# Attention scores of two heads side by side on TensorE's row halves, and a finer interleave of projections with the attention steps

## The chip, the cores and the metric

One Trainium2 chip, one of its cores. The metric is the device time of one execution in microseconds (us); the kernel before has a median of 945.48 us over 3 runs (945.21 to 947.18).

## The reference, cut to what matters

The kernel computes a decoder trunk of two layers on 256 tokens with 1024 channels. Each layer is a half-step SwiGLU, a mixer of three branches, and a second SwiGLU; the change lies in the mixer.

```python
h = rms_norm(x, norm_mix[l])
qa, ka, va, qb, kb, vb, xc, gc = _split_cols(h @ w_in[l])
# A: 4 query heads, 2 key heads of 64 channels, window 128, a sink per head
out_a = swa_sink_mixer(rope(qa), rope(ka), va, attn_sinks[l])
# B: 6 heads of 64 channels, three dilated windows joined by their denominators
out_b = dilated_mixer(rope(qb), rope(kb), vb)
# C: conv(4) -> gated linear recurrence, times gelu(gc)
out_c = rglru_mixer(xc, gc, conv_w[l], ..., positions)
x = x + concat(out_a, out_b, out_c) @ w_out[l]
```

In A and B every head computes `softmax(q k^T * scale + mask) v`, with 64 channels in the product q k^T.

## The kernel before, in words

All weights come as float32. `piece` (L123) loads a piece over SP's DMA queue, and splits it into two parts: ScalarE (ACT) makes `hi` (L130), VectorE (DVE) makes `lo` (L132). The same split is made of the activations by `split` (L135). Every product with weights is three TensorE (PE) matmuls in the one-pass format fp32r: hi x hi, hi x lo, lo x hi (L427 to L430 in `mac`, L461 to L463 in the SwiGLU, L704 to L706 in `project_T`, L938 to L940 in `out_stage`). Seven pieces fit in the ring of hi and lo tiles (tag "w", 14 tiles), so a new hi waits for the matmuls of the seventh piece before it.

What is computed inside the attention is plain float32, which the trace shows as two PE records for each matmul: the scores (L826), the product with the values (`o`, L856), and the recurrence gates (`gate_c`, L738). Transposes (`pT` L850, `qkT` L805, `gT` L437) are one record each.

One layer's mixer takes these steps, and the string `PLAN` (L20) is the order in which they are recorded:

- `xc`, `qb`, `kb`, `vb`, `pa`, `gc`: projections of the normed input: C's input, B's queries, keys and values, A's queries with keys and values, C's gate. They use 24 matmuls of 256 columns for each third of 384 channels (xc, gc), or 48 of 384 (qb, kb, vb) or 512 columns (pa).
- `cg`, `cs`, `co`: the gates, the scan and the output of C.
- `B0s0`, `A1s1` and so on: the scores of one group of heads for token half 0 or 1 (128 queries against 128 or 256 keys). `p` steps transpose the exponentials (pT), copy them out of PSUM on ACT (L657) and multiply with the values (o). `f` (`finish`, L859) divides by the sum, transposes (gT) and splits the result into `parts` (hi on ACT L136, lo on DVE L137).
- `woB`, `woCA`: the output projection over B's channels, then over C's and A's, in two halves of 512 output channels each (the loop over `c` in `out_stage`, L924), added to x by DVE (L943).

Behind the scores of a head stands a chain: DVE adds the mask and takes the maximum (L830), makes the negative maximum (L834, L836), ACT takes the exponential with the row sum (L839), and PE transposes. A head's 64 channels lie on one half of the partitions: even heads of B and key head 0 of A on partitions 0 to 63, the others on 64 to 127. Before, a group of scores is one bank of PSUM and holds heads of one half only:

```python
for g in range(2):
    for i0 in range(0, NP, per):
        heads.append([hd(2 * i + g) for i in range(i0, min(i0 + per, NP))])
```

A scheduler takes the recorded order as a priority and moves an instruction ahead where its inputs and its buffers allow. Each engine then runs its own list strictly in order. PSUM has 8 banks: 4 with the tag "mm", 2 "at", 2 "tp" (transposes).

Of the kernel before, what the change touches and what calls it, by code (L numbers as in the profile page):

```python
# [38 lines left out]
def hybrid_trunk(ctx: ExitStack, tc: tile.TileContext, a: dict, out: bass.AP):  # L39
# [393 lines left out]
    def gT(h, g, n, hi, lo):  # L433

        ps = bank("tp", "gT")
        for j in range(n // P):
            nc.tensor.transpose(ps[:, j * P:(j + 1) * P], g[:, j * P:(j + 1) * P], ident)  # L437
        split(hi, lo, ps[:, :n].rearrange("p (k t) -> p k t", t=P))
# [198 lines left out]
    def mixer(l, norm, nxt):  # L637
# [46 lines left out]

        def project(o, n, name):
            bs = None
            for k, w in w_in_pieces(o, n):
                if bs is None:
                    bs = [bank("mm", name)[:, :n] for _ in range(NH)]
                with behind_stats(k):  # L690
                    mac([(k, [(norm.parts(h, k), [(bs[h], w)]) for h in range(NH)])], KD)
            return bs

        def project_T(o, n, name, tags):

            bs = None
            for k, (wh, wl) in w_in_pieces(o, n):
                if bs is None:
                    bs = [bank(t, name)[:, :S] for t in tags]
                xh, xl = (norm.both(k)[:, o:o + S] for o in (0, S))  # L700
                with behind_stats(k):
                    for i, b in enumerate(bs):
# [3 lines left out]
                        nc.tensor.matmul(b, wj, xh, start=False, stop=(k == KD - 1))  # L706
# [13 lines left out]
        def c_conv():  # L720
            xc = project_T(oC, CW, "xc", TAG_XC)
# [41 lines left out]
        def c_gelu():  # L763
            gc = project_T(oC + CW, CW, "gc", TAG_GC)
# [3 lines left out]
            A.activation(ge, ge, AF.Gelu_apprx_tanh)  # L768
# [31 lines left out]
        def q_k(ps, h, nh, dst, groups=None):  # L800
            r = rope(ps, h, nh, groups)
            n = nh * HD // P
            tp = bank("tp", "qkT")
            for c in range(n):
                nc.tensor.transpose(tp[:, c * P:(c + 1) * P], r[:, c * P:(c + 1) * P], ident)  # L805
            copy("qk", dst[:, :, h * P:(h + 1) * P], tp[:, :n * P].rearrange("p (c t) -> p c t", c=n))

        class Attend:


            def __init__(self, h, heads, vs, mask, sinks):
                self.h, self.heads, self.vs, self.mask, self.sinks = h, heads, vs, mask, sinks
                self.nk = (h + 1) * P
                self.nh = sum(len(b) for b in heads)
                st = act.tile([P, 4, 8], F32, tag="st", bufs=4, name="st")
                self.mx, self.nm, self.ls, self.ri = (st[:, i] for i in range(4))
                self.slot = [sum(len(b) for b in heads[:i]) for i in range(len(heads))]
                self.sm = [None] * len(heads)
                self.ob = None

            def scores(self, gi):
                group, j, nk, mx, nm = self.heads[gi], self.slot[gi], self.nk, self.mx, self.nm
                h, n = self.h, len(group)
                sb = bank(TAG_SCORES, "scores")
                for s, (i, g, q, k) in enumerate(group):
                    nc.tensor.matmul(sb[:, s * nk:(s + 1) * nk], q[g * HD:(g + 1) * HD, h * P:(h + 1) * P],  # L826
                                     k[g * HD:(g + 1) * HD, :nk], start=True, stop=True)
                sm = act.tile([P, 512], F32, tag="sm", bufs=NSM, name="sm")
                for s in range(n):
                    V.tensor_tensor_reduce(out=sm[:, s * nk:(s + 1) * nk], in0=sb[:, s * nk:(s + 1) * nk],  # L830
                                           in1=self.mask, scale=1.0, scalar=NEG, op0=ALU.add, op1=ALU.max,
                                           accum_out=mx[:, j + s:j + s + 1])
                if self.sinks is None:
                    V.tensor_scalar(nm[:, j:j + n], mx[:, j:j + n], -SC, None, op0=ALU.mult)  # L834
                else:
                    V.scalar_tensor_tensor(nm[:, j:j + n], mx[:, j:j + n], -SC, self.sinks[1][:, j:j + n],  # L836
                                           op0=ALU.mult, op1=ALU.min)
                for s in range(n):
                    A.activation(sm[:, s * nk:(s + 1) * nk], sm[:, s * nk:(s + 1) * nk], AF.Exp, scale=SC,  # L839
                                 bias=nm[:, j + s:j + s + 1], accum_out=self.ls[:, j + s:j + s + 1])  # L840
                self.sm[gi] = sm

            def pv(self, gi):
                h, sm = self.h, self.sm[gi]
                if self.ob is None:
                    self.ob = bank(TAG_O, "o")
                tp = bank("tp", "pT")
                n = len(self.heads[gi]) * self.nk
                for b in range(n // P):
                    nc.tensor.transpose(tp[:, b * P:(b + 1) * P], sm[:, b * P:(b + 1) * P], ident)  # L850
                pT = act.tile([P, 512], F32, tag="pT", bufs=2, name="pT")
                copy("pT", pT[:, :n], tp[:, :n])
                for s, (i, g, q, k) in enumerate(self.heads[gi]):
                    for kb in range(h + 1):
                        b = s * (h + 1) + kb
                        nc.tensor.matmul(self.ob[:, i * HD:(i + 1) * HD], pT[:, b * P:(b + 1) * P], self.vs[kb][i],  # L856
                                         start=(kb == 0), stop=(kb == h))

            def finish(self):  # L859
# [7 lines left out]
                order = [i for group in self.heads for i, *_ in group]  # L867
# [155 lines left out]
```

## Time and profile before

| | us |
|---|---|
| median of 3 runs | 945.48 |
| the profiled execution: its own time | 946.71 |
| its span, first to last instruction | 944.9 |
| PE busy in the span | 935.2 (99%) |
| DVE busy | 662.1 (70%) |
| ACT busy | 502.0 (53%) |
| mean granted PE clock | 0.996 of full speed |

The two mixers lie at about 192 to 291 us and 654 to 753 us of the span. In them DVE is the fullest engine beside PE: the profile's stretches of 5 us show it busy for 5.00 of 5 us from 220 to 235 us, and for 2.30 of 5 us from 255 to 260 us. A busy time of PE is the sum of records whose ends are modelled: a matmul of 256 columns is shown as 0.28 us long although the next one starts 0.11 us later. So costs on PE are read from the distance of starts, and not from the length of a record.

### The profile page before, as it was taken

The numbers are of one execution on the slowest core, as the hardware profiler recorded it, in microseconds if no ns is written. First come the engines' busy times: TensorE is split into PE (matmuls) and PEld (weight loads), VectorE is DVE, ScalarE is ACT, GpSimd is POOL, SyncE is SP. The second block draws the span as 40 slices with busy tenths as digits, with TensorE's granted clock in tenths as the row PEclk, the third lists the DMA queues.
The fourth block names the chain that finished last, engine by engine and source line by source line (L and its number), as shares of the span: only waits on it lengthen the run. The fifth ranks groups of instructions, "written<-read, shape, count | busy, mean of one in ns | idle before, by whom it ended". The sixth has DMA issues, their size and how long they took to land.

```text
span 944.9 us, 18771 instructions
## 1 busy us (share of the span) xinstructions
PE 935.2 (99%) x7572; PEld 910.7 (96%) x7572; DVE 662.1 (70%) x1155; ACT 502.0 (53%) x769; POOL 59.8 (6%) x107
## 2 busy tenths in 40 slices
PE   8999999999999999999999999999999999999997
PEld 8999999999899999999999999999988999999886
DVE  6786675989678867765577766565995975656544
ACT  7554554455667545555355555544475675555530
POOL 4000001011102000001000000011100100000000
PEclk9999999999999999999999999999999999999999
DMA  8876665655246666565746666654741755666631
GB/s 279 238 227 206 191 197 162 195 175 166 79 132 214 178 205 198 180 216 165 223 157 200 194 205 203 202 180 119 224 138 50 229 178 180 196 207 201 201 112 44
DMA packets 134408, 171.13 MB, mean 181 GB/s; under 512 B 5822, under 2 KB 106258, under 8 KB 134322
## 3 DMA queue, kind: packets, MB, share of 16 engines
q1 hardware_dynamic: 133184, 168.32, 58.0%
q0 software_dynamic: 528, 0.57, 0.4%
q8 instruction: 59, 0.97, 0.4%
q10 hardware_dynamic: 608, 1.06, 0.4%
q14 instruction: 29, 0.22, 0.1%
HBM read 168.88 MB, written 1.05 MB: 180 GB/s over the span
## 4 chain that ended last, share of the span: by engine, by line
PE 97%; issue 1%; DMA 1%; SPq 0%; DVE 0%; POOLq 0%; POOL 0%
PE gate L461 9%; PE gate L462 9%; PE gate L463 8%; PE up L462 8%; PE up L463 8%; PE up L461 8%; PE down L461 6%; PE down L463 6%; PE down L462 6%; PE down L609 2%; PE down L608 2%; PE down L607 2%; PE scores L826 2%; PE wout L938 2%; PE wout L939 2%; PE wout L940 2%
## 5 line engine op out<-in xcount | busy, mean ns | idle before, releaser
L132 DVE TENSOR_TENSOR lo<-raw,hi 128x1024 fp32r<-128x1024 f32 (+2 forms) x334 | 388.8, 1173 | 113.7 <-ACT hi L130 113.3
L130 ACT ACTIVATE hi<-raw 128x1024 fp32r<-128x1024 f32 (+2 forms) x334 | 335.5, 1017 | 167.4 <-PE down L462 60.9
L461 PE MATMUL gate<-x,hi 128*128 128x256 f32 x704 | 195.8, 278 | 0.5 <-ACT x L372 0.5
L462 PE MATMUL gate<-x,hi 128*128 128x256 f32 x704 | 195.1, 277 | 0.0
L461 PE MATMUL up<-x,hi 128*128 128x256 f32 x704 | 194.6, 277 | 0.0
L462 PE MATMUL up<-x,hi 128*128 128x256 f32 x704 | 194.5, 277 | 0.0
L463 PE MATMUL gate<-x,lo 128*128 128x256 f32 x704 | 194.5, 277 | 0.0
L463 PE MATMUL up<-x,lo 128*128 128x256 f32 x704 | 194.1, 276 | 0.0
L461 PE MATMUL down<-g,hi 128*128 128x256 f32 x528 | 145.8, 276 | 0.0
L462 PE MATMUL down<-g,hi 128*128 128x256 f32 x528 | 145.7, 276 | 0.0
L463 PE MATMUL down<-g,lo 128*128 128x256 f32 x528 | 145.6, 276 | 0.0
L461 PEld LDWEIGHTS gate<-x,hi 128*128 128x128 f32 x704 | 132.6, 188 | 0.7 <-ACT x L372 0.7
L462 PEld LDWEIGHTS gate<-x,hi 128*128 128x128 f32 x704 | 132.8, 189 | 0.0
L462 PEld LDWEIGHTS up<-x,hi 128*128 128x128 f32 x704 | 132.4, 188 | 0.0
L463 PEld LDWEIGHTS gate<-x,lo 128*128 128x128 f32 x704 | 132.3, 188 | 0.0
L461 PEld LDWEIGHTS up<-x,hi 128*128 128x128 f32 x704 | 132.3, 188 | 0.0
L463 PEld LDWEIGHTS up<-x,lo 128*128 128x128 f32 x704 | 132.0, 188 | 0.0
L136 ACT ACTIVATE g<-gu 128x256 fp32r<-128x256 f32 x88 | 36.6, 417 | 149.3 <-DVE gu L475 125.4
L461 PEld LDWEIGHTS down<-g,hi 128*128 128x128 f32 x528 | 99.1, 188 | 0.1
L462 PEld LDWEIGHTS down<-g,hi 128*128 128x128 f32 x528 | 99.1, 188 | 0.0
L463 PEld LDWEIGHTS down<-g,lo 128*128 128x128 f32 x528 | 99.0, 188 | 0.0
L474 DVE TENSOR_TENSOR gu<-up,half 128x256 f32<-128x256 f32 x66 | 27.7, 421 | 47.1 <-PE up L463 47.1
(228 smaller groups left out, 1325.5 us busy)
## 6 DMA issues: line engine op xcount, KB each, us to landing
raw<-ffn_down SPq DMA_DIRECT2D x88, 512.0 KB, 4.5
raw<-ffn_gate SPq DMA_DIRECT2D x87, 512.0 KB, 4.7
raw<-ffn_up SPq DMA_DIRECT2D x87, 512.0 KB, 5.2
raw<-w_in SPq DMA_DIRECT2D x40, 384.0 KB, 3.7
raw<-w_out SPq DMA_DIRECT2D x12, 512.0 KB, 3.7
raw<-w_in SPq DMA_DIRECT2D x8, 512.0 KB, 4.6
raw<-w_out SPq DMA_DIRECT2D x8, 256.0 KB, 2.8
xr<-x SPq DMA_DIRECT2D x4, 256.0 KB, 4.6
```

The costliest lines, as they stand in the source:

```text
L130: nc.scalar.activation(hi[:, :m], raw[:, :m], AF.Copy)
L132: nc.vector.tensor_tensor(lo[:, :m], raw[:, :m], hi[:, :m].bitcast(F32), op=ALU.subtract)
L136: nc.scalar.activation(hi, v, AF.Copy)
L461: nc.tensor.matmul(b, wh, both[:, :S], start=first, stop=False)
L462: nc.tensor.matmul(b, wh, both[:, S:], start=False, stop=False)
L463: return nc.tensor.matmul(b, wl, both[:, :S], start=False, stop=last)
L474: V.tensor_tensor(u, bs[1], half, op=ALU.mult)
L607: nc.tensor.matmul(b, gh, wh, start=first, stop=False)
L608: nc.tensor.matmul(b, gh, wl, start=False, stop=False)
L609: return nc.tensor.matmul(b, gl, wh, start=False, stop=last)
L826: nc.tensor.matmul(sb[:, s * nk:(s + 1) * nk], q[g * HD:(g + 1) * HD, h * P:(h + 1) * P], k[g * HD:(g + 1) * HD, :nk], start=True, stop=True)
L938: nc.tensor.matmul(bs[j], wi, PT[:, k, 0], start=(i == 0), stop=False)
```

## The change

- **Scores by pairs.** `Attend` takes steps in place of groups. A step has two banks, one for each half of the partitions, and its matmuls are recorded in turn: a head of the lower half, one of the upper half, and so on. B has one step for half 0 (6 heads) and two for half 1 (4 and 2 heads); A has one step for each half (4 heads). The exponentials are laid out by head number in tiles of 512 columns, so `finish` needs no reordering, and the negative maximum is taken once for a step.
- **Steps cut finer.** `p` now only transposes and copies, `o` multiplies with the values, `aT` transposes A's rotated queries and keys. `project`, `project_T` and `out_stage` are generators, so one projection can be recorded in parts between other steps. `gl` is the gelu of C's gate, which was part of `gc`.
- **Order.** `behind(C["pe"])` holds matmuls and transposes of the attention behind the last projection matmul recorded before them. `PLAN` now has A's projection (`pa`) ahead of B's values (`vb`), and parts of `pa`, `vb`, `gc` and `wo` between the steps of the attention.
- **Banks.** `o` moves from the tag "at" to "mm", C's gate projection to "mm" alone, and the output projection to two "mm" and two "at" banks.

The arithmetic is unchanged. The core of the diff:

```diff
-PLAN = ("xc qb kb cg B1s0 vb B0s0 B0s1 B0p0 B0p1 pa B1s2 B1s1 cs A0s0 B1s3 B1p0 B0f A0s1 B1p2 B1p1 A1s0 B1p3 "
-        "A1s1 A0p1 A0p0 gc A1p0 B1f woB A1p1 A0f A1f co woCA").split()
-TAG_GATE, TAG_SCORES, TAG_O, TAG_WO = 'at', 'at', 'at', 'mm'
-TAG_XC, TAG_GC = ('mm', 'at', 'mm'), ('at', 'mm', 'mm')
+PLAN = ("xc qb kb cg pa pa pa B0s0 pa B1s0 vb B0p0 B0p1 B1s1 cs vb aT0 vb aT1 A0s0 vb gc B0o0 B0o1 B1p0 B1p1 "
+        "gc B1o0 B1o1 B1p2 B0f gc B1o2 A0p0 A1s0 gc gl A0o0 B1f A1p0 A1p1 woB A1o0 A1o1 A0f woB A1f co "
+        "woCA woCA woCA woCA").split()
+TAG_GATE, TAG_SCORES, TAG_O, TAG_WO = 'at', 'at', 'mm', ('mm', 'mm', 'at', 'at')
+TAG_XC, TAG_GC = ('mm', 'at', 'mm'), ('mm', 'mm', 'mm')
...
         def project(o, n, name):
             bs = None
             for k, w in w_in_pieces(o, n):
+                if k and k % 2 == 0:
+                    yield
...
             def scores(self, gi):
-                group, j, nk, mx, nm = self.heads[gi], self.slot[gi], self.nk, self.mx, self.nm
-                h, n = self.h, len(group)
-                sb = bank(TAG_SCORES, "scores")
-                for s, (i, g, q, k) in enumerate(group):
-                    nc.tensor.matmul(sb[:, s * nk:(s + 1) * nk], q[g * HD:(g + 1) * HD, h * P:(h + 1) * P],
-                                     k[g * HD:(g + 1) * HD, :nk], start=True, stop=True)
...
+                (banks, tiles), nk, mx, nm, h = self.steps[gi], self.nk, self.mx, self.nm, self.h
+                sb = [bank(TAG_SCORES, "scores") for _ in banks]
+                at = {}
+                for s in range(max(len(b) for b in banks)):
+                    for t, group in zip(sb, banks):
+                        if s < len(group):
+                            i, g, q, k = group[s]
+                            at[i] = t[:, s * nk:(s + 1) * nk]
+                            with behind(C["pe"]):
+                                nc.tensor.matmul(at[i], q[g * HD:(g + 1) * HD, h * P:(h + 1) * P],
+                                                 k[g * HD:(g + 1) * HD, :nk], start=True, stop=True)
...
+            def pT(self, gi):
+                sm, heads = self.sm[gi]
+                tp = bank("tp", "pT")
+                n = len(heads) * self.nk
+                for b in range(n // P):
+                    with behind(C["pe"]):
+                        nc.tensor.transpose(tp[:, b * P:(b + 1) * P], sm[:, b * P:(b + 1) * P], ident)
+                pT = act.tile([P, 512], F32, tag="pT", bufs=2, name="pT")
+                copy("pT", pT[:, :n], tp[:, :n])
+                self.p[gi] = pT
...
         def b_attend(h, q, k):
             hd = lambda i: (i, i % 2, q[:, i // 2], k[:, i // 2])
             per = 512 // ((h + 1) * P)
-            heads = []
-            for g in range(2):
-                for i0 in range(0, NP, per):
-                    heads.append([hd(2 * i + g) for i in range(i0, min(i0 + per, NP))])
-            return Attend(h, heads, vb, K["mB"][h], None)
+            steps = []
+            for i0 in range(0, NP, per):
+                pairs = range(i0, min(i0 + per, NP))
+                banks = [[hd(2 * i + g) for i in pairs] for g in range(2)]
+                idx = range(2 * i0, 2 * pairs[-1] + 2)
+                steps.append((banks, [list(idx[i:i + per]) for i in range(0, len(idx), per)]))
+            return Attend(h, steps, vb, K["mB"][h], None)
```

How the instructions now stand, at two places (layer 0; layer 1 has the same order). A row is a line of the kernel, the operation, output<-inputs with the buffer's number, and the shape; `xN` is N of them in a row.

**Place 1: PE, B's first scores.** Before, inside A's projection; the two tiles hold heads of the lower half only:

```order
L430 MATMUL pa_3086<-hi_3075,x_2019 128x512
L826 MATMUL scores_2944<-mixed_2597 128x256 x2
L826 MATMUL scores_3031<-mixed_2597 128x128 x3
L427 MATMUL pa_3087<-hi_3075,x_2019 128x512
L428 MATMUL pa_3087<-lo_3076,x_2019 128x512
```

Now all six heads of half 0 stand together, scores_3006 of the lower and scores_3007 of the upper half:

```order
L431 MATMUL pa_2957<-hi_2983,x_2522 128x512
L849 MATMUL scores_3006<-mixed_2597 128x128
L849 MATMUL scores_3007<-mixed_2597 128x128
L849 MATMUL scores_3006<-mixed_2597 128x128
L849 MATMUL scores_3007<-mixed_2597 128x128
L849 MATMUL scores_3006<-mixed_2597 128x128
L849 MATMUL scores_3007<-mixed_2597 128x128
L428 MATMUL pa_2956<-hi_2989,x_2522 128x512
```

The halves now take turns. In the whole mixer the scores stand in 9 unbroken runs before and in 7 now: B half 0 (the six above); B half 1, four in turn; the last two heads of B half 1, each alone between projections; A half 0 in the order lower, lower, upper, upper; A half 1, three in turn; and its last head alone.

**Place 2: PE, ACT and DVE, from B's last result to the output projection.** PE before: behind the transpose of B's result for half 1 (gT_3431) come one pair of transposes and 24 matmuls of gc, and only then wout:

```order
L850 MATMUL pT_3417<-ident_67,sm_3276 128x128 x2
L437 MATMUL gT_3431<-ident_67,o_3429 128x128 x3
L850 MATMUL pT_3417<-ident_67,sm_3276 128x128 x2
L704 MATMUL gc_3325<-x_2019,hi_3314 128x256
L705 MATMUL gc_3325<-x_2019,hi_3314 128x256
L706 MATMUL gc_3325<-x_2019,lo_3315 128x256
```

PE now: behind the same transpose (gT_3406) come four products of A and four transposes:

```order
L721 MATMUL gc_3235<-x_2522,lo_3301 128x256
L439 MATMUL gT_3406<-ident_67,o_3404 128x128 x3
L887 MATMUL o_3398<-va_3041,pT_3357 128x64 x4
L874 MATMUL pT_3412<-ident_67,sm_3365 128x128 x4
L971 MATMUL wout_3438<-parts_2598,hi_3427 128x256
L971 MATMUL wout_3439<-parts_2598,hi_3427 128x256
L971 MATMUL wout_3440<-parts_2598,hi_3427 128x256
L971 MATMUL wout_3441<-parts_2598,hi_3427 128x256
L874 MATMUL pT_3419<-ident_67,sm_3366 128x128 x4
L972 MATMUL wout_3438<-parts_2598,hi_3427 128x256
```

ACT now, where L866 is the exponential, L131 a weight's hi and L137 the hi of `parts`:

```order
L866 ACTIVATE sm_3365,st_3062<-sm_3365,st_3062 128x256 x2
L866 ACTIVATE sm_3366,st_3062<-sm_3366,st_3062 128x256 x2
L894 ACTIVATE st_3062<-st_3062 128x4
L131 ACTIVATE hi_3585<-raw_3584 128x1024
L137 ACTIVATE parts_2598<-gT_3406 128x3x128
L1014 ACT_TABLE_LOAD
```

DVE now, where L782 are C's gate products, L898 the division of A's half 0, L133 a weight's lo and L138 the lo of `parts`:

```order
L782 TENSOR_TENSOR ge_2599<-gc_3235,rows_2704 128x256
L898 TENSOR_TENSOR o_3495<-o_3398,st_3061 128x256
L895 TENSOR_TENSOR st_3062<-st_3062 128x4
L896 RECIPROCAL st_3062<-st_3062 128x4
L133 TENSOR_TENSOR lo_3586<-raw_3584,hi_3585 128x1024
L138 TENSOR_TENSOR parts_2598<-gT_3406,parts_2598 128x3x128
```

The first four wout matmuls read the hi of `parts`, the row L972 its lo; both now stand on ACT and DVE behind the exponentials of A's half 1 and behind a weight piece.

## Rows read from the trace of the kernel before

**Rows 1.** The page: busy times by engine, then the chain's shares.

```profile
PE 935.2 (99%) x7572; PEld 910.7 (96%) x7572; DVE 662.1 (70%) x1155; ACT 502.0 (53%) x769; POOL 59.8 (6%) x107
...
PE 97%; issue 1%; DMA 1%; SPq 0%; DVE 0%; POOLq 0%; POOL 0%
```

**Rows 2.** All waits of PE: who waited <- for whom: us, times, longest.

```profile
PE warm L115 <- POOL ident masks.py:199: 1.4, 1, 1.4
PE xT L367 <- DMA xr<-x: 1.1, 1, 1.1
PE gate L461 <- ACT x L372: 0.5, 1, 0.5
```

**Rows 3.** Groups by line: PE's scores (busy us, mean ns, idle before).

```profile
L826 PE MATMUL scores<-mixed 64*128 64x256 f32 (+1 forms) x80 | 17.8, 347 | 0.0
```

**Rows 4.** Timeline of PE (start, length): one score of 256 keys alone.

```profile
253.43 0.28 PE L706 MATMUL gc<-x,lo 128*128 128x256 f32 x1
253.63 0.70 PE L826 MATMUL scores<-mixed 64*128 64x256 f32 x2
254.26 0.39 PE L704 MATMUL gc<-x,hi 128*128 128x256 f32 x1
254.48 0.28 PE L705 MATMUL gc<-x,hi 128*128 128x256 f32 x1
```

**Rows 5.** The chain in order of time (start us, us, what): small PE work.

```profile
223.82 0.43 PE gate_c L738 x2
...
252.56 0.44 PE pT L850 x4
...
265.07 0.33 PE gT L437 x3
...
277.22 0.84 PE o L856 x8
```

**Rows 6.** Timeline of PE: from B's last transpose to the output projection.

```profile
264.90 0.49 PE L437 MATMUL gT<-ident,o 128*128 128x128 f32 x3
...
265.37 0.36 PE L704 MATMUL gc<-x,hi 128*128 128x256 f32 x1
...
268.16 0.28 PE L706 MATMUL gc<-x,lo 128*128 128x256 f32 x1
268.28 0.63 PE L938 MATMUL wout<-parts,hi 128*128 128x256 f32 x4
```

**Rows 7.** ACT in 192:300, groups by line and shape (busy, mean ns, idle).

```profile
L130 ACT ACTIVATE hi<-raw 128x1024 fp32r<-128x1024 f32 x19 | 19.5, 1052 | 7.4 <-PE pb L428 3.6 <-PE wout L939 3.3 <-ACT hi L130 0.2
L839 ACT ACTIVATE sm<-sm,st 128x256 f32<-128x256 f32 x10 | 5.0, 502 | 5.7 <-DVE st L834 5.7
L839 ACT ACT_TABLE_LOAD x1 | 1.3, 1283 | 0.0
L136 ACT ACTIVATE parts<-gT 128x384 fp32r<-128x384 f32 x2 | 1.0, 492 | 1.5 <-PE gT L437 1.5
```

**Rows 8.** DVE in 192:300, groups by line and shape.

```profile
L132 DVE TENSOR_TENSOR lo<-raw,hi 128x1024 fp32r<-128x1024 f32 x18 | 22.3, 1254 | 2.1 <-ACT hi L130 2.1
L830 DVE CUSTOM_DVE_ANT_0 sm<-scores,mA 128x256 f32<-128x256 f32 x4 | 1.5, 422 | 1.5 <-PE scores L826 1.5
L137 DVE TENSOR_TENSOR parts<-gT,parts 128x384 fp32r<-128x384 f32 x2 | 1.1, 558 | 0.6 <-ACT parts L136 0.6
L869 DVE TENSOR_TENSOR o<-o,st 128x256 f32<-128x256 f32 x2 | 0.8, 418 | 0.3 <-issue 0.3
```

**Rows 9.** Timeline of PE: two stretches of wout, first and last row each.

```profile
272.65 0.28 PE L938 MATMUL wout<-parts,hi 128*128 128x256 f32 x1
...
274.01 0.28 PE L938 MATMUL wout<-parts,hi 128*128 128x256 f32 x1
...
287.01 0.28 PE L938 MATMUL wout<-parts,hi 128*128 128x256 f32 x1
...
290.19 0.28 PE L938 MATMUL wout<-parts,hi 128*128 128x256 f32 x1
```

More of the change, by code (lines that the diff above doesn't have):

```diff
@@ L431, in mac, with gT @@
         return last
[L433 removed]
+    def gT(h, g, n, hi, lo, after=None):
         ps = bank("tp", "gT")
         for j in range(n // P):
[L437 removed]
+            with behind(after):
+                nc.tensor.transpose(ps[:, j * P:(j + 1) * P], g[:, j * P:(j + 1) * P], ident)
         split(hi, lo, ps[:, :n].rearrange("p (k t) -> p k t", t=P))
@@ L683, in behind_stats, with whole @@
             return behind(C.get("stats"))
+        def whole(g):
+            while True:
+                try:
+                    next(g)
+                except StopIteration as e:
+                    return e.value
         def project(o, n, name):
@@ L690, in project @@
                 with behind_stats(k):
-                    mac([(k, [(norm.parts(h, k), [(bs[h], w)]) for h in range(NH)])], KD)
+                    C["pe"] = mac([(k, [(norm.parts(h, k), [(bs[h], w)]) for h in range(NH)])], KD)
             return bs
@@ L813, in __init__ @@
                 self.nk = (h + 1) * P
-                self.nh = sum(len(b) for b in heads)
+                self.nh = sum(len(b) for banks, _ in steps for b in banks)
                 st = act.tile([P, 4, 8], F32, tag="st", bufs=4, name="st")
                 self.mx, self.nm, self.ls, self.ri = (st[:, i] for i in range(4))
-                self.slot = [sum(len(b) for b in heads[:i]) for i in range(len(heads))]
-                self.sm = [None] * len(heads)
+                self.sm, self.p = [], {}
@@ L843, in pv @@
             def pv(self, gi):
-                h, sm = self.h, self.sm[gi]
+                h, (_, heads), pT = self.h, self.sm[gi], self.p[gi]
                 if self.ob is None:
                     self.ob = bank(TAG_O, "o")
[L847 to L851, printed above, removed]
@@ L852, in pv @@
-                copy("pT", pT[:, :n], tp[:, :n])
-                for s, (i, g, q, k) in enumerate(self.heads[gi]):
+                for s, i in enumerate(heads):
                     for kb in range(h + 1):
                         b = s * (h + 1) + kb
-                        nc.tensor.matmul(self.ob[:, i * HD:(i + 1) * HD], pT[:, b * P:(b + 1) * P], self.vs[kb][i],
-                                         start=(kb == 0), stop=(kb == h))
+                        with behind(C["pe"]):
+                            nc.tensor.matmul(self.ob[:, i * HD:(i + 1) * HD], pT[:, b * P:(b + 1) * P],
+                                             self.vs[kb][i], start=(kb == 0), stop=(kb == h))
@@ L931, in out_stage @@
                 w = list(w.items())
-                bs = [bank(TAG_WO, "wout")[:, :S] for _ in range(KC)]
+                bs = [bank(TAG_WO[j], "wout")[:, :S] for j in range(KC)]
                 order = [(i, j) for i in range(n - LO) for j in range(KC)]
                 order += [(i, j) for j in range(KC) for i in range(n - LO, n)]
-                for i, j in order:
+                for ij, (i, j) in enumerate(order):
+                    if ij and ij == (n - LO) * KC:
+                        yield
                     k, (wh, wl) = w[i]
@@ L950, in out, with go_on @@
         def out(stage):
-            out_stage([R[m] for m in stage], stage == PLAN[-1][2:])
+            return out_stage([R[m] for m in stage], stage == PLAN[-1][2:])
+        running = {}
+        def go_on(step, start):
+            if step not in running:
+                running[step] = start()
+            next(running[step], None)
         for step in PLAN:
```

91 lines of the change are left out of this document (51 added, 40 removed).

## The prediction

> **What bounds the kernel now.** I read the page first. PE is busy for 99% of the span and is 97% of the chain that ended last [rows 1], so the end moves only if PE has less to do or is made to wait. The waits view then says whether it waits: three times in the whole program, 3.0 us in all, and all three at the very start [rows 2]. In neither mixer does PE wait for anyone as far as the records show, and no load of w_in or w_out is among the releasers. Since a record's end is modelled, I checked this with the distances of starts. A score of 256 keys costs two records (80 for 40 heads [rows 3]), a float32 matmul of 256 columns 0.43, four transposes 0.44 or three 0.33, four products with the values 0.84 [rows 5]. Added up over the mixer, such prices leave no gap over about 0.2 us at one place. So the attention already costs what PE's work in it costs: nothing is hidden that an interleave could uncover, and only the scores get cheaper. What the interleave can do is go wrong.
>
> One thing PE pays for that is no arithmetic: around a lone score of 256 keys, the starts from the gc matmul ahead to the second gc matmul behind are 254.48 - 253.43 = 1.05 us apart [rows 4]. Two steps of gc are 0.23 of it (such a matmul takes 0.113 to 0.118 [rows 9]), the score's columns 0.43 (the price of gate_c, of the same columns on all 128 rows [rows 5]). The other 0.39 is paid for going into the 64-row form and out of it. The score itself, on half the rows, streams no faster than a matmul on all of them.
>
> Durations below come from the profiled execution, which took 946.71 us with a span of 944.9; it lies 0.13% above the median of 945.48. I work out differences from it and put them on the median. About 0.2% (1.9 us) is what a measurement of this kernel can tell from no change.
>
> **Fewer runs of scores.** 9 runs a layer become 7. At 0.39 each that is 0.78 a layer, -1.6 us for both. I take it whole, since a run pays on the two sides whatever it holds.
>
> **Overlap of the halves.** Per layer the scores have 6x128 + 6x256 + 4x128 + 4x256 = 3840 columns, at 0.43 / 256 that is 6.45 us. No run of scores in the kernel before holds heads of both halves, so no row shows whether two of them run at once. One bound is nothing gained. For the other I count with two rules: a head's two records follow each other on its half, and records start in program order, but the next one may start beside the last if its half is free. A record is then 0.107 (128 keys) or 0.213 us (256), and n heads in turn take 2n + 1 steps in place of 4n/2 x 2: the six heads of B half 0 take 7 for 12 (saved 5 x 0.107 = 0.54), the four of half 1 take 5 for 8 (3 x 0.213 = 0.64), A half 0 in the order lower, lower, upper, upper 7 for 8 (0.11), the three of A half 1 take 4 for 6 (0.43). The three heads that stand alone save nothing. Sum 1.72 a layer, -3.4 us for both. I take this end: the two sets of rows, and the two banks written, have nothing in common, and rows 4 show that a score occupies the array's time for its columns, whichever half it leaves empty.
>
> On the loss side, a change of half inside a run may cost like the entry of a run; that is a rival below. The Trainium skill (TensorEngine Tiling (Array Packing), Key Properties) says that changing the tiling mode drains TensorE, while changing only the tile does not. The 0.39 of rows 4 agrees with the first half; no row here shows the second. By that rule the sum below stands as it is; if a change of half cost the 0.39 of the rows too, it would be the last rival's.
>
> **Out-projection, woB.** Here I find a wait that was not there. T is the end of A's last lone score on PE. Before, 24 gc matmuls stood between B's transpose and wout: 265.37 to 268.28 [rows 6], 2.9 us in which ACT (0.49) and DVE (0.56) made `parts`. Now there are four products (0.84) and four transposes (0.44).
> PE: 18 gc at 0.115 = 2.1, gT 0.33, o 0.84, pT 0.44, so it asks for wout at T + 3.7.
> ACT: the exponentials need the one negative maximum of all four heads, so they begin after DVE's last maximum (0.42) and some 0.2 of small steps, at T + 0.7; four take 4 x 0.50 [rows 7], to T + 2.7, one small exponential to T + 2.9, then the weight piece hi_3585 at 1.05 to T + 3.9, then the hi of `parts` 0.49 to T + 4.4. PE waits 0.7 and runs four wout matmuls (0.46), to T + 4.85.
> DVE: o_3495 waits for the four products (T + 3.3), 0.42, two small ones 0.3, lo_3586 1.25 to T + 5.3, the lo of `parts` 0.56 [rows 8] to T + 5.8. It holds up pT_3419 too, whose bank is the one that gT_3406 leaves. PE waits another 0.95.
> That is about 1.6 a layer; durations on ACT and DVE overlap a little at their ends, so I take 1.5, +3.0 us for both. Ends: none if the two engines come through earlier, 2.2 a layer if one more small step is late on each.
>
> **First exponentials.** B half 0's now stand on ACT behind two table loads (1.28 each [rows 7]), a square root and two weight pieces that wait for PE's last pa matmuls, and pT_3106 follows after 12 + 13 vb and one run of scores. My walk along ACT gives a margin between -0.4 and +0.7 us. I take 0.2 a layer, +0.4 us; ends 0 and 0.8.
>
> **Pace of the 256-column matmuls.** In one stretch of wout 12 matmuls take 274.01 - 272.65 = 1.36 (0.113 each), in a later one 27 take 290.19 - 287.01 = 3.18 (0.118) [rows 9]. Small work between seems to set which pace follows; I don't know the rule. Some 220 matmuls a layer ran at the slow pace and 57 of wout at the fast. All slow would cost 0.3 a layer, all fast would gain 1.0; I take the middle, -0.7 us for both.
>
> **Costs nothing.** The moved banks: `o` needs an "mm" bank that values or B's division leave; between those and its use stand 3 to 4 us of other PE work (22 gc at 0.115 for B half 1). The values' copies have 4 us from the last vb matmul to the first `o`. A's rotation and POOL's additions end some 8 us ahead of `aT0`. On SP's queue four loads of A's weights move ahead of vb's; PE waits for none of these loads now [rows 2], and hi pieces wait for PE instead. DVE has a few small maxima fewer and no reordering; PE's work covers that, it gives nothing. The cover is gone only where `parts` is late, above. The gelu apart from gc puts a table load behind the hi of `parts` and ahead of pT_3417's copy, which PE asks for 3.7 us later.
>
> **Sum.** -1.6 - 3.4 + 3.0 + 0.4 - 0.7 = -2.3 us, 945.5 - 2.3 = **943.2 us**.
>
> **The rivals.**
> *No wait at woB.* If ACT and DVE run further ahead than I walk them, 3.0 + 0.4 less one small rest fall away: -5.3, 940.2 us. For it: DVE had idle time in the attention before, 2.7 us of the 5 from 255 to 260. Against: the order of the rows on ACT and DVE is fixed. 0.17.
> *The halves do not overlap.* Only the runs count: -1.6 + 3.0 + 0.4 - 0.7 = +1.1, 946.6 us. For it: no row shows overlap. 0.15.
> *The halves are independent of program order.* Each half streams its own heads: B half 0 6 steps, B half 1 4, A half 0 4: another 0.64 a layer, 1.3 less: 941.9 us. For it: nothing in the rows; against: everything else on PE starts in order. 0.10. The Trainium skill (TensorEngine Tiling (Array Packing), Theoretical Speedup) gives up to 2x for 64 rows, which is this case where both halves are full; no run here shows it.
> *Weight loads set the pace.* Four products of 64 columns take 0.84, 0.21 each [rows 5], twice their columns' 0.107: loading float32 weights for a record takes about 0.105. If loads for the two halves go one after the other, records of 128 keys (0.107) gain nothing, those of 256 all: 0.65 a layer is lost again: -2.3 + 1.3 = -1.0, 944.5 us. 0.10.
> *A change of half costs like an entry.* The runs hold 5 + 3 + 1 + 2 = 11 changes a layer, 22 in all. At 0.39 they cost 8.6 us on top of the case without overlap: +9.7, 955.2 us. It decides for slower from 0.04 us a change (1.1 + 22 x 0.04 = 2.0). For it: rows 4, an entry does cost that. Against: within a run the form stays one of 64 rows. 0.08.
>
> **How the numbers follow.** My forecast has 0.40 and a range of its own of 941.5 to 945 (the pace and the wait at woB, 1 us each way). The range of 940.0 to 948.0 reaches from the case without the wait to the case without overlap and with a longer wait; outside are the costly change of half and a part of the first rival. Faster than 943.6: 0.25 of the forecast's 0.40, 0.13 of the first rival, 0.08 of the independent halves, 0.02 of the weight loads: 0.48. Slower than 947.4: 0.08, a third of the case without overlap (0.05) and the upper ends of the forecast and the weight loads with still more waits: 0.18. The rest, 0.34, is no change that can be told.
>
> **What would show it.** Scores of the two halves that start less than 0.2 us apart in the six heads of B half 0, which then last about 0.75 us plus 0.39 (serial: 1.3 plus 0.39). Seven runs of scores. Waits of PE in the mixer that the waits view did not have: wout or pT behind ACT's and DVE's `parts`, 0.5 to 1 us each, twice a layer. The forecast is wrong if PE waits elsewhere for more than 1 us, if wout starts behind gT without a gap, or if a run with both halves takes longer than its columns and 0.39.

## The result, and the profile after

The changed kernel takes 954.01 us (median of 4 runs, 953.09 to 954.38) against 946.14 for the one before: ratio 1.0085, 95% interval 1.0073 to 1.0097. It is slower, by 0.85%; the forecast was 943.2 us, and the time lies outside the range.

The profiled execution took 953.84 us with a span of 952.1, 7.2 longer than before. The page, busy times by engine and the chain's shares (to [rows 1]):

```profile
PE 937.5 (98%) x7572; PEld 913.3 (96%) x7572; DVE 660.1 (69%) x1145; ACT 501.4 (53%) x765; POOL 64.2 (7%) x107
...
PE 96%; ACT 1%; issue 1%; DMA 1%; DVE 0%; SPq 0%; POOLq 0%; POOL 0%
```

PE is still the bound, with as many records as before, and ACT has 1% of the chain. All waits of PE after (who waited <- for whom: us, times, longest; to [rows 2]):

```profile
PE pT L874 <- ACT pT L659: 3.8, 2, 1.9
PE wout L971 <- ACT parts L137: 1.5, 2, 0.7
PE warm L116 <- POOL ident masks.py:199: 1.4, 1, 1.4
PE xT L368 <- DMA xr<-x: 1.0, 1, 1.0
PE gate L463 <- ACT x L373: 0.3, 1, 0.3
```

The first two are new, 5.3 us, each once a layer. To find the rest I cut the span where PE sums the squares of each norm (`rms`); columns are us between those starts on PE's timeline:

| | up to the first | mixer 0 | layer 0, second SwiGLU | layer 1, first SwiGLU | mixer 1 | rest |
|---|---|---|---|---|---|---|
| before | 196.27 | 102.75 | 180.24 | 179.00 | 102.78 | 183.86 |
| after | 194.82 | 103.12 | 180.37 | **185.82** | 104.03 | 183.94 |
| gc_hold (below) | 194.19 | 98.66 | 180.36 | 185.82 | 98.58 | 183.89 |
| hold_one_one (below) | 194.70 | 98.68 | 180.37 | 179.92 | 98.67 | 183.96 |

So 6.8 of the 7.2 us lie in a stage that the change does not touch, and 1.6 in the two mixers. The start is 1.5 shorter, which is no gain of the change: in the profiled execution before, the granted clock was at 0.50 from about 10 to 13 us, in that of the changed kernel at 1.00. A stretch of each, before and then after (us; busy us of PE, PEld, DVE, ACT, POOL; the granted clock as a share of 2.4 GHz; DMA):

```profile
11.00:12.00 1.00, 1.00 (x7) 1.00 (x6) 0.80 (x3) 0.84 (x1) 0.00 (x0) 0.50 1.05 366
```

```profile
11.00:12.00 1.00, 1.00 (x12) 1.00 (x11) 1.00 (x3) 0.85 (x1) 0.00 (x0) 1.00 0.98 302
```

Both starts occur in other kernels below (0.50 again in gelu_late and hold_one), so a median holds some of each; without the start the stages grow by 8.65 us.

**The SwiGLU of layer 1.** PE's groups by form (busy us, mean ns, idle before), before in 484 to 658 us, and after in 483 to 664:

```profile
L461 PE MATMUL down<-g,hi 128*128 128x256 f32 x176 | 48.6, 276 | 0.0
L461 PE MATMUL up<-x,hi 128*128 128x256 f32 x164 | 45.3, 276 | 0.0
```

```profile
L463 PE MATMUL down<-g,hi 128*128 128x256 f32 x176 | 49.5, 281 | 0.0
L463 PE MATMUL up<-x,hi 128*128 128x256 f32 x164 | 46.1, 281 | 0.0
```

Same matmuls, same order, no idle time; yet each record is 5 ns longer. By starts, 1536 steps take 664.01 - 483.11 = 180.90 us after (0.1178 each) and 658.15 - 484.05 = 174.10 before (0.1133). These are the two paces of [rows 9], now over a whole stage. I call them the 281 ns and the 276 ns pace.

**The mixers.** PE after, from B's last transpose to the output projection, layer 0 (start, length; to [rows 6]):

```profile
261.94 0.49 PE L439 MATMUL gT<-ident,o 128*128 128x128 f32 x3
262.26 1.00 PE L887 MATMUL o<-va,pT 128*128 128x64 f32 x8
263.10 0.61 PE L874 MATMUL pT<-ident,sm 128*128 128x128 f32 x4
264.44 0.74 PE L971 MATMUL wout<-parts,hi 128*128 128x256 f32 x4 [0.73 <-ACT parts L137]
267.08 1.12 PE L874 MATMUL pT<-ident,sm 128*128 128x128 f32 x4 [1.90 <-ACT pT L659]
267.85 0.56 PE L972 MATMUL wout<-parts,hi 128*128 128x256 f32 x1
268.21 0.42 PE L973 MATMUL wout<-parts,lo 128*128 128x256 f32 x1
268.42 0.41 PE L971 MATMUL wout<-parts,hi 128*128 128x256 f32 x1
```

ACT in the same stretch:

```profile
262.97 1.04 ACT L131 ACTIVATE hi<-raw 128x1024 fp32r<-128x1024 f32 x1
263.92 0.47 ACT L137 ACTIVATE parts<-gT 128x384 fp32r<-128x384 f32 x1
264.40 1.28 ACT L1014 ACT_TABLE_LOAD   x1
265.70 0.84 ACT L1014 ACTIVATE ge<-ge 128x768 f32<-128x768 f32 x1
266.45 0.58 ACT L659 ACTIVATE pT<-pT 128x512 f32<-128x512 f32 x1
```

The second group of pT (267.08) starts when ACT has copied the first one out of PSUM (266.45 + 0.58), and that copy stands behind the table load and the gelu. Behind the wait, matmuls start 0.21 us apart and not 0.12. The same in stretches (columns as above):

```profile
264.00:266.00 2.00, 0.74 (x4) 0.53 (x4) 1.74 (x3) 1.97 (x4) 0.00 (x0) 1.00 0.00 0
266.00:267.00 1.00, 0.00 (x0) 0.00 (x0) 0.43 (x1) 1.00 (x2) 0.00 (x0) 0.70 0.40 60
267.00:268.00 1.00, 0.92 (x5) 0.92 (x6) 0.53 (x1) 0.03 (x1) 0.00 (x0) 0.50 0.97 323
268.00:269.00 1.00, 1.00 (x6) 1.00 (x6) 0.00 (x0) 0.70 (x2) 0.00 (x0) 0.50 0.49 158
269.00:270.00 1.00, 1.00 (x7) 1.00 (x6) 0.34 (x1) 0.62 (x1) 0.00 (x0) 0.59 0.00 0
270.00:275.00 5.00, 5.00 (x46) 5.00 (x45) 3.77 (x7) 1.83 (x3) 0.00 (x0) 1.00 0.00 0
...
738.00:739.00 1.00, 1.00 (x6) 1.00 (x6) 0.82 (x2) 0.36 (x1) 0.00 (x0) 0.50 0.00 0
```

From 264 to 267 PE had worked 0.74 us; then the granted clock was at 1.2 GHz, until about 269.8. What is missing from 1.00 while PE works adds up to 1.4 us here (0.50 + 0.50 + 0.41) and 1.7 in layer 1 (737 to 742). With the 5.3 of idle time the two places cost 8.4 us. The clock's part is not fixed: in the profiled execution of after_one_one (below), with the same two waits in both layers, the clock read 0.50 until about 272.4 us in layer 0 and 1.00 throughout in layer 1, and the mixers took 104.34 and 101.72 us.

**The scores.** Groups by line after (to [rows 3]), and B half 0's run of twelve records with its neighbours:

```profile
L849 PE MATMUL scores<-mixed 64*128 64x128 f32 (+1 forms) x80 | 12.0, 352 | 0.0
```

```profile
228.64 0.94 PE L849 MATMUL scores<-mixed 64*128 64x128 f32 x12
229.50 0.50 PE L428 MATMUL pa<-hi,x 128*128 128x512 f32 x1
```

The run lasts 229.50 - 228.64 = 0.86 us. That is as long as six records of one half took before:

```profile
240.55 0.93 PE L826 MATMUL scores<-mixed 64*128 64x128 f32 x6
241.41 0.50 PE L428 MATMUL pa<-lo,x 128*128 128x512 f32 x1
```

In the trace, where each record has its own start, the twelve begin in six pairs, 6 or 7 ns apart; the first step is 0.21 us, the others 0.11, and 0.20 passes from the last pair to the next matmul, as it does behind a run of one half. So the two halves run side by side from the first record on. The others agree: the eight records of B half 1 take 1.06 us where four of one half took 1.06 before, and A half 0, recorded lower, lower, upper, upper, takes 0.65 for its eight where four took 0.64; its upper half starts 13 ns behind its lower. From each run's first start to the next other matmul, the nine runs of a layer sum to 8.3 us before and the seven to 5.5 after: 2.8 a layer gained.

### The profile page after: what moved, and what is told of

It is laid out like the page before. It is cut to its first block, busy times and chain, and to the rows that moved or that the text cites. A ratio compares the mean times of both kernels' runs of the same rounds, so it can differ in the third digit from the quotient of the medians.

```text
span 952.1 us, 18757 instructions
## 1 busy us (share of the span) xinstructions
PE 937.5 (98%) x7572; PEld 913.3 (96%) x7572; DVE 660.1 (69%) x1145; ACT 501.4 (53%) x765; POOL 64.2 (7%) x107
## 3 DMA queue, kind: packets, MB, share of 16 engines
q10 hardware_dynamic: 608, 1.06, 0.3%
## 4 chain that ended last, share of the span: by engine, by line
PE 96%; ACT 1%; issue 1%; DMA 1%; DVE 0%; SPq 0%; POOLq 0%; POOL 0%
PE gate L463 9%; PE gate L465 8%; PE up L465 8%; PE gate L464 8%; PE up L464 8%; PE up L463 8%; PE down L463 6%; PE down L465 6%; PE down L464 6%; PE down L611 2%; PE down L610 2%; PE down L609 2%; PE wout L972 2%; PE wout L973 2%; PE wout L971 2%; PE o L887 1%
## 5 line engine op out<-in xcount | busy, mean ns | idle before, releaser
L133 DVE TENSOR_TENSOR lo<-raw,hi 128x1024 fp32r<-128x1024 f32 (+2 forms) x334 | 388.5, 1172 | 119.8 <-ACT hi L131 116.9
L131 ACT ACTIVATE hi<-raw 128x1024 fp32r<-128x1024 f32 (+2 forms) x334 | 336.8, 1017 | 180.8 <-PE down L464 64.2
L137 ACT ACTIVATE g<-gu 128x256 fp32r<-128x256 f32 x88 | 36.6, 417 | 148.1 <-DVE gu L477 124.2
```

What stands on the lines that cost most here:

```text
L131: nc.scalar.activation(hi[:, :m], raw[:, :m], AF.Copy)
L133: nc.vector.tensor_tensor(lo[:, :m], raw[:, :m], hi[:, :m].bitcast(F32), op=ALU.subtract)
L137: nc.scalar.activation(hi, v, AF.Copy)
```

## The experiments

Theory 1: the changed kernel loses 8.4 us at woB and 6.8 to the pace of layer 1's SwiGLU, which small work in PE's stream sets and the attention's arithmetic does not. Rival: the finer interleave itself costs.

**gelu_late.** The gelu of C's gate held behind ACT's two copies of pT; PE's order unchanged.

```diff
...
-                A.activation(out, in_, AF.Copy, **({} if s is None else {"scale": s}))
+                C["copy"] = A.activation(out, in_, AF.Copy, **({} if s is None else {"scale": s}))
...
-                A.activation(C["ge"], C["ge"], AF.Gelu_apprx_tanh)
+                with behind(C["copy"]):
+                    A.activation(C["ge"], C["ge"], AF.Gelu_apprx_tanh)
```

> The gelu of C's gate is held behind both pT copies of A's half 1; PE's order is that of the changed kernel. Theory 1 (two causes: PE's waits at woB with the half clock that follows them, and the slow pace of layer 1's first SwiGLU): the second wait (3.8 us in the two layers, PE pT <- ACT pT) falls to some 0.8, because the copy of pT comes 2.1 us (table load 1.28 and gelu 0.84) earlier; the granted clock stays at 1.0 behind it, which gives back some 2.5 us; so 954.0 - 3.0 - 2.5 = 948.5 us if the SwiGLU keeps its 281 ns records, 941.7 if it turns to 276 ns (6.8 us less). Rival (the finer interleave itself costs, by more switches on PE): the wait's idle time goes, but the time stays above 951. Rival (the second wait is for the lo of parts, as predicted): it keeps at least 1.5 us a layer.

948.24 us (ratio to before 1.0034, 1.0012 to 1.0056), as expected for the 281 ns pace, which the SwiGLU kept. Waits of PE:

```profile
PE wout L971 <- ACT parts L137: 1.5, 2, 0.7
...
PE wout L972 <- DVE parts L138: 0.4, 2, 0.2
```

The wait of pT is gone, and what I had forecast in its place, the lo of `parts`, is 0.2 a layer. The second group of pT now starts ahead of DVE's lo of `parts`, so its bank was not the one that gT_3406 leaves:

```profile
266.41 0.60 PE L874 MATMUL pT<-ident,sm 128*128 128x128 f32 x4
```

```profile
266.58 0.55 DVE L138 TENSOR_TENSOR parts<-gT,parts 128x384 fp32r<-128x384 f32 x1
```

The clock reads 1.00 in every stretch from 260 to 275 us: the waits of 0.73 and 0.18 that are left did not lower it. The two mixers take 100.05 and 99.96 us, 7.2 less than in the changed kernel; the medians differ by 5.8.

**gc_hold.** As gelu_late, with the last 18 gc matmuls held behind B's last transpose.

```diff
...
-        "gc B1o0 B1o1 B1p2 B0f gc B1o2 A0p0 A1s0 gc gl A0o0 B1f A1p0 A1p1 woB A1o0 A1o1 A0f woB A1f co "
-        "woCA woCA woCA woCA").split()
...
+        "aT1 A0s0 vb gc B0o0 B0o1 B1p0 B1p1 gc B1o0 B1o1 B1p2 B0f gc B1o2 A0p0 A1s0 A0o0 "
+        "B1f gc A1p0 A1p1 gl woB A1o0 A1o1 A0f woB A1f co woCA woCA woCA woCA").split()
...
-                with behind_stats(k):
+                with behind_stats(k), behind(C["gT"] if name == "gc" and k >= KD - 2 else None):
```

> As gelu_late, and the last 18 gc matmuls are held behind B's last transpose, so that they stand between it and wout, as 24 did in the kernel before. Theory 1: PE waits neither for parts nor for pT (all of 5.3 us of idle time and 2.8 of half clock gone): 954.0 - 8.1 = 945.9 us with 281 ns records in layer 1's first SwiGLU, 939.1 with 276 ns. Rival (interleave costs): above 950 in either case. In every case the waits view has only its three entries at the start.

943.78 us (0.9993, 0.9976 to 1.0010), 2.1 below the expectation. The waits are the three of the start:

```profile
PE warm L116 <- POOL ident masks.py:199: 1.4, 1, 1.4
PE xT L368 <- DMA xr<-x: 0.6, 1, 0.6
PE gate L464 <- ACT x L373: 0.5, 1, 0.5
```

The mixers are 4.1 and 4.2 us shorter than before (table). So the interleave costs nothing that shows once nothing waits; layer 1's first SwiGLU still takes 185.82.

**serial_halves.** The changed kernel, lower half first, then upper.

```diff
-                for s in range(max(len(b) for b in banks)):
-                    for t, group in zip(sb, banks):
+                for t, group in zip(sb, banks):
+                    for s in range(max(len(b) for b in banks)):
```

> The changed kernel with the heads of a step recorded lower half first, then upper half, and not in turn: the same seven runs of scores, the same instructions. By the count of 2n + 1 (each half runs its own records one after the other, records start in order) B half 0 takes 11 record times for 7, B half 1 7 for 5, A half 1 5 for 4 (the heads in the run may change): 0.43 + 0.43 + 0.21 = 1.1 a layer, 2.1 us for both: 956.1 us, if the pace of the SwiGLUs does not turn; the run of twelve records at 228.6 lasts 0.43 longer. If the halves don't overlap at all: 954.0 and a run of the same length. If the halves were independent of program order: 954.0 and the same length, shorter than 12 record times.

957.28 us (1.0125, 1.0110 to 1.0140). B half 0:

```profile
228.94 1.26 PE L849 MATMUL scores<-mixed 64*128 64x128 f32 x12
230.13 0.50 PE L428 MATMUL pa<-hi,x 128*128 128x512 f32 x1
```

1.19 us and not 0.86: the halves overlap still, but for a part. By the starts in the trace the upper half's first record begins beside the third of the lower half's six (229.270 and 229.264), 0.33 us behind the first, and takes 0.86 from there. The 0.43 expected by the count of 2n + 1 came near for another reason: if PE's list has the records as they are recorded, and each had to start behind those ahead of it, the upper half could not have begun before the lower's sixth. So a half that is recorded second starts at once where four records of the other stand ahead of it (A half 0), and two record times late where six do; what sets this is not shown. B half 1 came out as two runs, one for each half, of 1.06 each, against 1.06 for all four heads; this was not expected, and is why more was lost than the 2.1 us expected (3.3 by the medians, 2.7 in the mixers of the profiled executions).

**probe_pace.** Transposes of the identity (nobody reads them) between the blocks of layer 1's first SwiGLU.

```diff
...
+                    if probes is not None and len(made) >= 4:
+                        with behind(mark):
+                            last = probe(PROBES[len(made) - 4])
...
```

> The changed kernel with 1, 2, 3 or 4 transposes of the identity (6 + 4 + 4 + 4 places, 42 in all, nobody reads them) ahead of 18 of the 22 gate and up blocks of layer 1's first SwiGLU. Cost of the places themselves: 42 x 0.11 and 18 x some 0.15 of switching, 7 us. If the pace is a state that interruptions of PE's stream can turn (theory 1): the stretches between the places run at 0.1133 or at 0.1178 us per matmul, with nothing between, and turn at some places. If the pace is a property of the stage or its data (rival): all stretches at 0.1178, and 961 us.

953.67 us in one run. Mean distance of starts in the stretch behind each place: 0.1178, 0.1135, 0.1178, 0.1178, 0.1135, 0.1178 behind six lone transposes; 0.1135 to 0.1139 behind all twelve groups of two to four. Nothing lies between; the 42 transposes cost about what the turned blocks gave back. The pace is a state, and a transpose can turn it.

**before_one, before_two.** The kernel before with one or two such transposes ahead of the fifth block; every other instruction in its place.

```diff
...
+                    if (l, i, len(made)) == (1, 1, 4):
+                        with behind(mark):
+                            for j in range(1):
+                                turn = nc.tensor.transpose(norm.rT[:, (2 + j) * P:(3 + j) * P], ident, ident)
...
```

> The kernel before with one transpose of the identity, whose result nobody reads, ahead of the fifth gate and up block of layer 1's first SwiGLU; every other instruction stands where it stood. Theory 1 (the pace is a state of PE's stream that a transpose can turn, and its price is the whole of 1392 matmuls x 0.0045 us): in the probe run a lone transpose turned 0.1135 to 0.1178 each time, so here the stretch behind it runs at 0.1178 and the time is 945.2 + 6.3 + 0.2 = 951.7 us. Rival (the slow stretch came from the attention's change, through its data or its waits): 945.4 us, records stay at 276 ns.

953.26 us (1.0093, 1.0061 to 1.0126); the stage from the sum of squares on takes 185.47 us against 179.00. PE ahead of the place (482 to 495 us) and behind it (495 to 663):

```profile
L461 PE MATMUL up<-x,hi 128*128 128x256 f32 x20 | 5.5, 276 | 0.0
```

```profile
L461 PE MATMUL up<-x,hi 128*128 128x256 f32 x144 | 40.5, 281 | 0.0
```

> As before_one with two transposes in a row, which in the probe run left a fast stretch fast. Theory 1: 945.2 + 0.4 = 945.6 us, 276 ns. If any interruption at this place turned the pace: 951.9.

945.46 us (0.9998, 0.9988 to 1.0007), 276 ns throughout. One transpose of 0.1 us makes the kernel before as slow as the changed one, two change nothing: the 281 ns stretch needs nothing of the change.

**after_two, hold_two, after_one, hold_one.** The same places in the changed kernel and in gc_hold.

> The changed kernel with two transposes at the same place, which in the probe run turned a slow stretch to fast. Theory 1: 954.0 - 6.3 + 0.4 = 948.1 us, records of the gate, up and down behind it at 276 ns. Rival (the slow stretch came from the attention's change itself): 954.4 us, 281 ns.

> gc_hold (the changed kernel without its waits) with the two transposes: both causes taken away. Theory 1: 943.8 - 6.3 + 0.4 = 937.9 us, faster than both kernels. Rival: 944.2.

> The changed kernel with one transpose at the fifth block. Theory 1: 954.0 - 6.3 + 0.2 = 947.9 us with records of 276 ns behind it, or 954.2 with 281 ns, and nothing between; the same side as hold_one if the turn depends on the order of PE's instructions alone, as that is the same from the sum of squares on.

> gc_hold with one transpose of the identity ahead of the fifth gate and up block of layer 1's first SwiGLU. In the probe run lone transposes gave slow, slow, fast, slow, slow, fast: two of three kinds of turn, so from a slow stretch one or two of them reach the fast one. Theory 1: either the stretch behind turns to 276 ns, 943.8 - 6.3 + 0.2 = 937.7 us, or it stays, 944.0; nothing between. Exactly one of this run and hold_one_one ends fast. Rival (the slow stretch belongs to the changed program, whatever interrupts it): 944.0 in both.

Medians 954.25, 944.41, 953.31 and 944.17 us; in all four the stretch stayed at 281 ns. Two transposes turned it in the probe run, where one stood at each of the six places ahead, and did not here. So the expectation was wrong for the two with two transposes: what a given group does depends on more than the pace ahead of it.

**hold_one_one, hold_rms, after_one_one.** A second lone transpose ahead of the sixth block; or, ahead of the fifth alone, four records of one column.

```diff
...
-                    bs[t] = banks(len(made))
+                    bs[t], at = banks(len(made)), (l, i) == (1, 1) and len(made) in (4, 5,)
+                    if at:
+                        with behind(mark):
+                            turn = nc.tensor.transpose(norm.rT[:, 2 * P:3 * P], ident, ident)
...
```

```diff
...
+                            for j in range(2):
+                                turn = nc.tensor.matmul(norm.rT[:, 2 * P + j:2 * P + j + 1], ident, ones, start=True, stop=True)
...
```

> gc_hold with a lone transpose ahead of the fifth and one ahead of the sixth block. Theory 1: 943.8 - 6.1 + 0.4 = 938.1 us if the first place leaves the stretch slow, 944 (less 0.2 for one fast block) if the first place has turned it.

938.13 us (0.9904, 0.9869 to 0.9938). PE between the two places, and behind the second:

```profile
L464 PE MATMUL up<-x,hi 128*128 128x256 f32 x8 | 2.2, 281 | 0.0
```

```profile
L464 PE MATMUL down<-g,hi 128*128 128x256 f32 x176 | 48.6, 276 | 0.0
```

> gc_hold with four records of one column (two float32 products with the ones, as the sum of squares has) at the fifth block. In the stages' own sums of squares such a group turned slow to fast in most runs of this case (664.13 in the changed kernel, 299.02 in the one before) and fast to slow in nearly all. Theory 1: 943.8 - 6.3 + 0.4 = 937.9 us if it turns, 944.2 if not.

938.25 us (0.9908, 0.9872 to 0.9943), turned at its one place. These two are faster than both kernels.

> The changed kernel, waits and all, with the two lone transposes that turned gc_hold to fast (fifth and sixth block). Theory 1: the turn depends on the order of PE's instructions, which is the same here, so the stretch behind the sixth block has 276 ns records: 954.0 - 6.1 + 0.4 = 948.3 us; what is left over the kernel before (945.4) is the waits at woB less the gain of the scores. If the stretch stays slow: 954.4.

947.51 us (1.0026, 1.0012 to 1.0040), turned at the same place as gc_hold: 6.5 us below the changed kernel from two transposes, 5.9 of it in that stage (179.93 against 185.82).

**hold_serial, old_order.** What the alternating order and the interleave are worth. hold_serial is hold_one_one with the loops of serial_halves; old_order has the steps in the order of the kernel before.

> hold_one_one with the heads of a step recorded lower half first, then upper half, as in serial_halves. There B half 0 took 0.33 longer, and B half 1 stood in two runs of one half each (0.64 less overlap and one more entry and exit, 0.39): 1.4 a layer, 938.1 + 2.8 = 940.9 us. If the overlap were worth nothing and only runs counted: 938.1 + 0.8 = 938.9.

941.21 us (0.9954, 0.9937 to 0.9970): recording the heads of B in turn, with the one run a layer that it saves, is worth 3.1 us. It is not all of the overlap, as A half 0 and a part of B half 0 overlap here too.

```diff
...
+PLAN = ("xc qb kb cg B1s0 vb vb vb vb B0s0 B0p0 B0o0 B0p1 B0o1 pa pa pa pa "
+        "aT0 aT1 B1s1 cs A0s0 B1p0 B1o0 B0f B1p1 B1o1 A1s0 B1p2 B1o2 A0p0 A0o0 gc gc gc "
+        "gc gl A1p0 A1o0 B1f woB woB A1p1 A1o1 A0f A1f co woCA woCA woCA woCA").split()
...
-                            with behind(C["pe"]):
+                            with behind(None):
...
```

> The changed kernel with the steps in the order of the kernel before, whole projections between them, and without holding the attention's matmuls behind the projections: scores by pairs alone. A step takes both banks for scores, so the next step's matmuls wait for DVE's maxima of the last (four at 0.42 us). If the finer interleave is what lets PE go on meanwhile: waits of PE at scores and pT, 3 us or more a layer, and a time above 950. If the interleave is worth nothing: about 941, as the scores' gain alone (2 x 2.8 us by the runs' lengths) would give.

998.08 us (1.0554, 1.0509 to 1.0600; 2 runs). Waits of PE, the first three:

```profile
PE scores L849 <- DVE st L858: 11.7, 4, 5.4
PE qkT L823 <- POOL r L809: 5.8, 2, 2.9
PE wout L971 <- ACT parts L137: 3.9, 2, 2.0
```

Both banks are held until DVE has all maxima, and with whole projections ahead PE has nothing else to do. The clock falls too, and by my estimate it is the larger part: the mixers are 25.7 and 23.3 us longer than before, and in them the granted clock was at 0.50 for some 41 and 34 us, 35 and 29 of them with PE busy, which at full clock would have taken half as long. With the interleave, and without the waits at woB, the change gains 8.3 us in the mixers; the pairs in the old order lose far more. Layer 1's first SwiGLU took 179.01 us here, at the 276 ns pace, with the scores by pairs: so the pairs by themselves do not bring the 281 ns pace.

## Why the prediction was wrong

- **Fewer runs, overlap of the halves:** -5.0 forecast; 2 x 2.8 = 5.6 found inside the runs. With the half of the 0.39 that lies ahead of a run and behind the next matmul, for two runs a layer, my estimate is 6.3 in all. The direction was right and the count of 2n + 1 was not: in the changed kernel B half 0 takes six record times, B half 1 four and A half 0 four, plus the 0.20 behind any run. That is the rival *independent of program order* (0.10, a gain 1.3 us larger than the forecast's); serial_halves shows that it has a limit. A change of half costs nothing that shows, as the Trainium skill (TensorEngine Tiling (Array Packing), Key Properties) has it for a change of tile alone: twelve records with five changes take no longer than six of one half. The rivals *halves do not overlap*, *weight loads set the pace* and *a change costs like an entry* fall.
- **Out-projection, woB:** forecast +3.0, found 8.4. The place and the first wait (0.7) were right. Two things failed. The second wait was put on the lo of `parts`, through the bank of gT_3406, at 0.95; PE waits for ACT's copy of pT_3412, 1.9. The sentence that failed is that the gelu "puts a table load behind the hi of `parts` and ahead of pT_3417's copy, which PE asks for 3.7 us later": PE's products ask for it later, but the next transposes need the bank that the copy frees, and they stand ahead of the rest of wout. gelu_late moves the gelu alone, and 5.8 us of the median go, 7.2 of the two mixers. And the wait was priced as idle time alone; the half clock behind it cost another 3.1 in this execution.
- **First exponentials:** +0.4 forecast; PE does not wait for pT there.
- **Pace of the 256-column matmuls:** -0.7 forecast, bounded at 0.3 and -1.0 a layer, because it was counted inside the mixer only. This is the step that failed most: the state lasts until the next interruption, so the stretch at stake was that of 1536 matmuls behind `rT` (two transposes of each norm, early in its stage), 6.8 us. Both paces were in [rows 9], and the text said that small work seems to set which follows; the bound had to be taken over all that follows.
- **The sum:** -5.6 + 8.4 + 6.8 is +9.6, and the span grew by 7.2. The half clock at the start of the execution before gives 1.5 of the difference, and some 1.2 is a further gain in the mixers, which gc_hold shows in full: 1.3 to 1.4 a layer beside the scores' 2.8. Of it 0.7 is the pace of gc and wout (steps of 0.1164 and 0.1167 on average before, 0.1142 and 0.1137 in gc_hold, some 240 matmuls), and an estimated 0.4 the two runs that are gone, outside of the runs themselves. The one rival on the slower side, 955.2 by a costly change of half, comes near the time for the wrong reason.

How far it is shown: a few dummy records turn the pace, and the median follows by 7.9 us (before_one), 6.0 (hold_one to hold_one_one) and 5.8 (after_one to after_one_one), the stage itself by 6.5, 6.0 and 6.0, where 1392 steps x 0.0045 make 6.3. That the waits make the rest is shown by gelu_late and gc_hold, 10.2 us in all, the pace of layer 1's wout among them. Why `rT` of layer 1 left the 281 ns pace behind in the changed kernel and the 276 ns pace in the one before, and in old_order, is not settled: what stands around it on PE is the same. So it is shown that the pace makes 6.8 us of the difference, and not that the change of the attention must bring it.

## What to carry to other kernels

Where a copy that frees a PSUM bank shares an engine with a table load, look who needs the bank next, not only who needs the copy; and price a wait of TensorE with the clock that may follow it (here 2.6 us of idle time were followed by a loss of 1.4 and 1.7 us in one execution, of some 2.6 and of nothing in another; 0.9 us by none). Heads of 64 channels on the two halves of the rows do overlap, in full when their records alternate; here it paid only where other work of PE stands between the steps that share their banks. And before a difference of under 1% is put down to an edit, compare the record lengths of stages that the edit does not touch.

## What the runs showed of the hardware

Two paces of the same matmuls, set by a state. The steps from start to start are 113, 113 and 114 ns in the kernel before (484 to 524 us), and 117 to 119 after: all steps of a stretch are longer, none stands out. Six lone transposes, 48 matmuls apart, gave 281, 276, 281, 281, 276, 281, as a counter of three would; groups of two to four did not follow it, and the rule is not shown. The pace can differ between executions of one program: the profiled one of after_one took 961.47 us (median 953.31), and there layer 0's first SwiGLU, too, ran at 281 ns. PE's groups from 30 to 160 us in it, and then in the changed kernel:

```profile
L464 PE MATMUL up<-x,hi 128*128 128x256 f32 x154 | 43.3, 281 | 0.0
```

```profile
L464 PE MATMUL up<-x,hi 128*128 128x256 f32 x152 | 42.0, 276 | 0.0
```
